# A decoder layer on one core: low halves on GpSimd in pieces of 256 columns, sums over partitions in fp32r

## The chip, the cores and the metric

The kernel runs on one core of a Trainium2 chip. The metric is the device time of one execution in microseconds; for each kernel the median of its runs is taken. The engines are named as in the profile: PE is TensorE, PEld its weight loads, DVE is VectorE, ACT is ScalarE, POOL is GpSimd, SP is SyncE.

## The reference

One layer of a decoder over 512 tokens of width 1024, batch 1, in float32: a gated mixer of NSA sparse attention (8 query heads, 2 key heads) and chunked GLA (4 heads), cross-attention to 256 memory tokens, a gated FFN with a three-tap convolution (width 2816), RMS norms between them and at the end. What the change touches:

```
def rms_norm(x, g):
    y = x * lax.rsqrt(jnp.mean(x * x, axis=-1, keepdims=True) + RMS_EPS)
    return y * g

# GLA: the decay of each key, from a rank-16 product; the norm of each head's output
log_a = jax.nn.log_sigmoid(a_low @ w_alpha2 + b_alpha) / 16.0     # (512,16) @ (16,256)
b = jnp.cumsum(log_a in chunks of 64)
...
o = o * lax.rsqrt(jnp.mean(o * o, axis=-1, keepdims=True) + RMS_EPS) * norm_g
```

## The kernel before

Activations lie transposed: 128 features on the partitions, 512 tokens in the free dimension. A product in float32 accuracy is made of three passes of fp32r matmuls (`mm3`, lines 160 to 162): each operand is split into a high half, its value rounded to fp32r, and a low half, the rest; the passes are high by high, high by low and low by high. A pass of 128 by 512 is one PE instruction.

**Weights.** All weights come as 141 blocks of 128 by 1024 in the order of use. `load_raw` (L126) issues a block's DMA on SP into one of 3 buffers. `convert` makes the two halves: the high half by a copy on ACT (L140), the low half by a subtraction (L141) on the engine that `lo_engine` names at that time. That is DVE at first; DVE and GpSimd in turn from L363 on (projections); DVE again from L452; GpSimd alone from L545 on (NSA and GLA stages with the dense products that fill them); DVE again from L882 (mixer's output and all behind it). Of the 141 blocks GpSimd makes 29. `take` converts two blocks ahead of the one in use.

**Splits of activations** are a copy on ACT (L165) and a subtraction on DVE (L166), by `split`.

**Stages.** First the projections ("proj"), then "nsa": for each of 8 pairs of key head and 128 queries, `nsa_scores` makes scores on PE, the row maxima on DVE, exponentials on ACT and the factors on DVE; `nsa_values` transposes and multiplies. Dense work that depends on none of it is put between them from the list `fillers` (stage name "fill"). The first filler is `gla_r(0)` with `gla_decay`. Then "gla": `gla_qk`, `gla_keys`, `gla_att`, `gla_states`, `gla_out` and `gla_norm` for 4 heads, again with fillers between them (`nsa_part`). Then "mix", "mkv", "wout", "xat", "xo", "up", "down", almost pure dense products.

**Order.** The source gives the semaphores and a priority; the order of the instructions within each engine is made by a list scheduler before the run, which places an instruction when its inputs are ready by its own estimates. Each engine then runs its list in that order. Dependences are kept by region of a tile: a matmul on columns 0 to 127 of a block waits for what wrote these columns.

**Sums over partitions.** A sum over the feature axis is a matmul with a 128 by 128 matrix of ones. `rstd_rows` (L237) does it for the norms ahead of "xat" and "up" (512 columns) and for the last norm (384 columns), `gla_norm` (L833) for each of the 4 GLA heads (512 columns): seven sums, each one fp32 matmul on the fp32 sum of squares. The sum of squares is collected by `add_square`: the square on ACT (L214), the addition on GpSimd (L224). In `gla_out` the square is L828 on ACT.

**The decay gate.** `gla_decay` transposes the 16 low-rank columns (L411), copies them from PSUM on DVE (L413), multiplies them in two fp32 matmuls of 16 by 512 (L418, m = 0 and 1), and goes on with L420 to L431 on ACT and DVE. Other DVE work in the same stretch: L316 and L332 (low halves of queries and keys), L603 (scaled row maxima), L627 (compressed scores times factor), L620 (factors on scores).

Of the kernel before, what the change touches and what calls it, by code (L numbers as in the profile page):

```python
# [9 lines left out]
F32 = mybir.dt.float32  # L10
F32R = mybir.dt.float32r
U32 = mybir.dt.uint32
AF = mybir.ActivationFunctionType
ALU = mybir.AluOpType
AX = mybir.AxisListType

P = 128
T = 512
# [40 lines left out]
def layer_kernel(ctx: ExitStack, tc: tile.TileContext, xT, memT, W, small, const, gfin, out, out_t, order):  # L59
    nc = tc.nc  # L60
# [5 lines left out]
    def sb(shape, dtype, tag, bufs):  # L66
        uid[0] += 1
        return pool.tile(shape, dtype, name=f"{stage[0]}_{tag}_{uid[0]}", tag=tag, bufs=bufs)
# [10 lines left out]
    def s_(dtype=F32):  # L79
        return sb([P, T], dtype, "s", SB)  # L80

    def t_(dtype=F32):
        return sb([P, T], dtype, "t", TB)
# [3 lines left out]
    def bank(tag):  # L87
        uid[0] += 1
        return psum.tile([P, T], F32, name=f"{stage[0]}_ps_{tag}_{uid[0]}", tag=tag, bufs=BANKS[tag])
# [14 lines left out]
    def C(name):  # L104
        a, b = CO[name]
        return cst[:, a:b]

    def S(name):
        a, b = SM[name]
        return sm[:, a:b]  # L110
# [7 lines left out]
    def halves(i):  # L118
        return [slice(0, T), slice(T, 1024)] if i < 4 else [slice(0, 1024)]

    def load_raw(upto):
        while emitted[0] <= min(upto, NBLK - 1):
            i = emitted[0]
            r = sb([P, 1024], F32, "raw", 3)
            for c in halves(i):
                nc.sync.dma_start(r[:, c], W[i][:, c])  # L126
            raws[i] = r
            emitted[0] += 1

    def convert(upto):  # L130
        while emitted[1] <= min(upto, NBLK - 1):
            i = emitted[1]
            load_raw(i + RAW_AHEAD)
            r = raws.pop(i)
            lo = lo_engine[i % len(lo_engine)]
            if i < NBLK - 8:
                wh = sb([P, 1024], F32R, "wh", 3)
                wl = sb([P, 1024], F32R, "wl", 3)
                for c in halves(i):
                    nc.scalar.activation(wh[:, c], r[:, c], AF.Copy)  # L140
                    lo.tensor_tensor(wl[:, c], r[:, c], wh[:, c].bitcast(F32), op=ALU.subtract)  # L141
                convs[i] = (wh, wl)
            else:
                tile_ = s_ if i < NBLK - 5 else g_
                convs[i] = []
                for c in (slice(0, T), slice(T, 1024)):
                    wh, wl = tile_(F32R), tile_(F32R)
                    nc.scalar.activation(wh, r[:, c], AF.Copy)
                    lo.tensor_tensor(wl, r[:, c], wh.bitcast(F32), op=ALU.subtract)
                    convs[i].append((wh, wl))  # L150
            emitted[1] += 1
# [12 lines left out]
    def split(h, l, src):  # L164
        nc.scalar.activation(h, src, AF.Copy)  # L165
        nc.vector.tensor_sub(l, src, h.bitcast(F32))  # L166
# [39 lines left out]
    def gain_split(k, src, gain):  # L206
        h, l = g_(F32R), g_(F32R)
        scaled_split(h, l, src, gain[:, k:k + 1])
        return h, l
# [16 lines left out]
    def rsqrt(dst, src, scale, refine=False):  # L226
        nc.scalar.activation(dst, src, AF.Sqrt, scale=scale, bias=C("eps"))
        nc.vector.reciprocal(dst, dst)
        if refine:
            v = sb([P, 4], F32, "newton", 2)[:, :dst.shape[-1]] if dst.shape[-1] <= 4 else t_()[:, :dst.shape[-1]]  # L230
            nc.vector.scalar_tensor_tensor(v, src, EPS / scale, dst, op0=ALU.add, op1=ALU.mult)
            nc.vector.scalar_tensor_tensor(v, v, -0.5 * scale, dst, op0=ALU.mult, op1=ALU.mult)
            nc.vector.scalar_tensor_tensor(dst, v, 1.5, dst, op0=ALU.add, op1=ALU.mult)

    def rstd_rows(sqacc, n=T, tag="o", refine=False):
        ps = bank(tag)
        nc.tensor.matmul(ps[:, :n], C("ones"), sqacc, start=True, stop=True)  # L237
        r = sb([P, T], F32, "rstd", 2)[:, :n]
        rsqrt(r, ps[:, :n], 1.0 / 1024, refine)
        return r  # L240
# [32 lines left out]
    ps = bank("o")  # L273
# [6 lines left out]
    for k in range(KT):  # L280
        r = s_()
# [3 lines left out]
            load_raw(k // 2)  # L285
    nc.sync.dma_start(cst, const)
    nc.sync.dma_start(sm[:, SM_GAINS:], small[:, SM_GAINS:])
    for k in range(KT):
        xg.append(gain_split(k, xr[k], S("ln_mix")))
        if k % 2 == 0 and k < 6:  # L290
            convert(k // 2)
        if k > 0:
            add_square(sqs, xr[k - 1], eng=nc.vector)
# [75 lines left out]
    for b0, nk in ((0, 3), (3, 3), (6, 2)):  # L369
        w = take(("BB", b0, nk))  # L370
        for j in range(nk):
            k = b0 + j
            c = slice(j * BW, (j + 1) * BW)
# [34 lines left out]
    def gla_decay():  # L408
        alT = bank("pt")
        for t in range(4):  # L410
            nc.tensor.transpose(alT[0:16, t * P:(t + 1) * P], alpha[t], C("ident"))  # L411
        als = t_()
        nc.vector.tensor_copy(als[0:16], alT[0:16])  # L413
        zs = []
        az = sb([P, 2, T], F32, "raw", 3)
        for m in range(2):
            ps = bank("pt")
            nc.tensor.matmul(ps, S("walpha")[0:16, m * P:(m + 1) * P], als[0:16], start=True, stop=True)  # L418
            z = t_()
            nc.scalar.activation(z, ps, AF.Identity, bias=S("b_alpha")[:, m:m + 1])  # L420
            nc.vector.scalar_tensor_tensor(az[:, m], z, -1.0, z, op0=ALU.mult, op1=ALU.max)
            zs.append(z)
        nc.scalar.activation(az, az, AF.Exp, scale=-1.0)
        nc.scalar.activation(az, az, AF.Ln, bias=1.0)
        for m in range(2):
            z = zs[m]
            nc.vector.scalar_tensor_tensor(z, z, 0.0, az[:, m], op0=ALU.min, op1=ALU.subtract)
            cs = g_()
            for c in range(8):
                v = slice(c * 64, c * 64 + 64)  # L430
                nc.vector.tensor_tensor_scan(cs[:, v], C("ones")[:, 0:64], z[:, v], 0.0, op0=ALU.mult, op1=ALU.add)  # L431
            cum[m] = cs
# [35 lines left out]
    for kv in range(2):  # L468
        nc.tensor.matmul(vps[0:31, kv * 64:(kv + 1) * 64], gTs[:, 62 + kv * 31:62 + (kv + 1) * 31], S("w2v"),
                         start=True, stop=True)  # L470
# [220 lines left out]
    for t in range(4):  # L691
        h, l = s_(F32R), s_(F32R)
# [114 lines left out]
    def gla_out(m, a, st, q2, a2):  # L807
        hd = 2 * m + a
        es = slice(hd * P, (hd + 1) * P)
        po = t_()  # L810
        for u in range(2):

            ps = bank(("o", "sc")[u]).rearrange("p (a n) -> p a n", a=2)
            for t in (2 * u, 2 * u + 1):
                ts = slice(t % 2 * P, (t % 2 + 1) * P)
                nc.tensor.matmul(ps[:, :, ts], vb[t][0][:, es], a2[u][:, :, ts], start=True, stop=False)
                nc.tensor.matmul(ps[:, 0, ts], vb[t][1][:, es], a2[u][:, 0, ts], start=False, stop=False)
                for c in (2 * t, 2 * t + 1):
                    if c == 0:
                        continue  # L820
                    cs = slice(c % 4 * 64, (c % 4 + 1) * 64)
                    s = st[(c - 1) // 4][:, (c - 1) % 4 * P:((c - 1) % 4 + 1) * P]
                    nc.tensor.matmul(ps[:, :, cs], s, q2[u][:, :, cs], start=False, stop=c % 2 == 1)
            pu = po[:, u * 256:(u + 1) * 256]
            nc.scalar.activation(pu, ps[:, 1], AF.Copy)
            nc.vector.tensor_add(pu, ps[:, 0], pu)
        sq = t_()
        nc.scalar.activation(sq, po, AF.Square)  # L828
        return hd, po, sq

    def gla_norm(hd, po, sq):
        pn = bank("pt")
        nc.tensor.matmul(pn, C("ones"), sq, start=True, stop=True)  # L833
        rs = t_()
        rsqrt(rs, pn, 1.0 / 128)
        og = t_()
        nc.vector.scalar_tensor_tensor(og, po, S("norm_g"), sr[hd], op0=ALU.mult, op1=ALU.mult)
        nc.vector.scalar_tensor_tensor(og, og, 0.5, rs, op0=ALU.mult, op1=ALU.mult)
        h, l = g_(F32R), g_(F32R)
        split(h, l, og)  # L840
        OG[hd] = (h, l)
# [31 lines left out]
    for k in range(KT):  # L873
        mr = t_()[:, :MEM]
        nc.sync.dma_start(mr, memT[:, k, :])
        hl = sb([P, 2, MEM], F32R, "s", SB)
# [9 lines left out]
    for n in range(0, 8, 2):  # L886
        th = [merge(C_MG, n, t_), merge(C_MG, n + 1, t_)]
        for j in range(2):
            ps = branch("w_branch_gla", OG, n + j)
            nc.vector.scalar_tensor_tensor(th[j], th[j], 1.0, ps, op0=ALU.add, op1=ALU.mult)  # L890
            nc.gpsimd.tensor_tensor(th[j], pm[n + j], th[j], op=ALU.add)
            if n < 4:
                x = pair()
                h, l = x[:, 0], x[:, 1]
            else:
                h, l = g_(F32R), g_(F32R)
# [9 lines left out]
    for hd in range(4):  # L906
        ps = pk[hd] if hd < 2 else dense8(("A", "w_xkv", hd * P), memg, MEM)
        kf = t_()[:, :MEM]
        nc.vector.tensor_mul(kf, ps[:, :MEM], rm)
        hl = sb([P, 2, MEM], F32R, "g", GB)  # L910
# [6 lines left out]
    for n in range(8):  # L917
        xr = t_()
        nc.sync.dma_start(xr, xT[:, n, :])
        ps = dense8(("A", "w_out", n * P), mix)  # L920
        r = g_()
# [9 lines left out]
    for t in range(2):  # L931
        h, l = g_(F32R), g_(F32R)
# [147 lines left out]
    for n in range(8):  # L1080
        ps = acc()
        for k in range(HF):
# [3 lines left out]
            c = slice(j % 8 * P, (j % 8 + 1) * P)  # L1086
# [42 lines left out]
    for n in range(4, 8):  # L1129
        ps = bank(("sc", "pt", "acc", "pt")[n - 4])[:, head]  # L1130
# [24 lines left out]
    for i, (h, c) in enumerate(((0, slice(0, T)), (1, slice(0, 256)), (1, slice(256, T)))):  # L1155
        ps = bank(("pt", "o", "sc")[i])[:, c]
# [141 lines left out]
```

## Time and profile before

| | us |
|---|---|
| runs shown | 873.52, 875.91, 876.02 |
| median | 875.91 |
| the profiled execution | 875.57 |
| its span on the core | 873.5 |
| PE busy | 853.2 |
| DVE busy | 557.7 |
| ACT busy | 419.1 |
| POOL busy | 214.2 |

The span runs from the first to the last instruction on the core; the execution's own time is 2.1 us longer. Busy time of PE counts each matmul to its modelled end, so neighbours overlap. A row of the timeline has the start, the duration (of several merged instructions from the first start to the last end), the engine, line, operation, tile written and tiles read, the shape and the count; in brackets stands idle time just ahead, with what ended it. An fp32 matmul shows as two entries. A DVE duration includes the time in which the instruction had been issued and could not yet start.

### The profile page before, as it was taken

What the parts mean: (1) busy time and instruction counts of PE and PEld (TensorE: products, weight loads), DVE (VectorE), ACT (ScalarE), POOL (GpSimd) and SP (SyncE); (2) the same over time, 40 slices, a digit from 0 to 9 for tenths busy, and PEclk for the clock granted to TensorE, in tenths of its full rate; (3) what the DMA queues carried; (4) which work ended last, traced back from release to release, by engine and by line L of the source; (5) the groups of instructions that cost most, each with busy time, mean ns of one, the idle gap of its engine ahead of it and who ended that gap; (6) DMA issues with size and microseconds to landing.
All of it is one profiled execution on the core that took longest, in us unless ns stands there. A gap on an engine that the chain in (4) does not pass through costs nothing.

```text
span 873.5 us, 11086 instructions
## 1 busy us (share of the span) xinstructions
PE 853.2 (98%) x4174; PEld 708.0 (81%) x4174; DVE 557.7 (64%) x908; ACT 419.1 (48%) x731; POOL 214.2 (25%) x160
## 2 busy tenths in 40 slices
PE   9999989999998999999999999999999999999996
PEld 6987777777786878898888788888888888888996
DVE  7576977998858378454487669665533465565324
ACT  7466767798445455344446535433311233334311
POOL 1373444344333314112300222111100111112121
PEclk9999999999999999999999999999999999999999
DMA  8333221002221232244341132322222223222302
GB/s 293 116 123 97 73 73 49 25 2 73 67 78 49 96 116 103 96 169 146 123 143 49 48 121 74 120 96 97 97 97 96 97 86 108 90 97 102 121 25 97
DMA packets 26406, 83.58 MB, mean 96 GB/s; under 512 B 3056, under 2 KB 5104, under 8 KB 26352
## 3 DMA queue, kind: packets, MB, share of 16 engines
q1 hardware_dynamic: 26064, 82.58, 27.2%
q8 instruction: 33, 0.54, 0.3%
q10 hardware_dynamic: 288, 0.28, 0.1%
q14 instruction: 21, 0.17, 0.1%
HBM read 80.76 MB, written 2.10 MB: 95 GB/s over the span
## 4 chain that ended last, share of the span: by engine, by line
PE 88%; DVE 7%; ACT 3%; issue 1%; POOL 1%; ACTq 0%; POOLq 0%
PE up_ps_sc L161 4%; PE up_ps_sc L160 4%; PE up_ps_sc L162 4%; PE fill_ps_acc L160 3%; PE fill_ps_acc L161 3%; PE fill_ps_acc L162 3%; PE up_ps_pt L160 3%; PE up_ps_pt L161 3%; PE up_ps_pt L162 3%; PE up_ps_acc L161 2%; PE up_ps_acc L160 2%; PE up_ps_acc L162 2%; PE nsa_ps_o L644 2%; PE down_ps_sc L162 2%; PE nsa_ps_pt L650 2%; PE down_ps_sc L161 2%
## 5 line engine op out<-in xcount | busy, mean ns | idle before, releaser
L1068 POOL TENSOR_TENSOR up_s<-up_s,up_s 128x512 f32<-128x512 f32 x22 | 35.8, 1630 | 259.6 <-ACT up_wh L140 207.7
L140 ACT ACTIVATE up_wh<-up_raw 128x1024 fp32r<-128x1024 f32 x40 | 42.5, 1062 | 64.9 <-PE up_ps_sc L161 33.0
L141 DVE TENSOR_TENSOR up_wl<-up_raw,up_wh 128x1024 fp32r<-128x1024 f32 x40 | 62.8, 1569 | 16.0 <-ACT up_wh L140 15.9
L141 POOL TENSOR_TENSOR fill_wl<-fill_raw,fill_wh 128x1024 fp32r<-128x1024 f32 x16 | 38.5, 2407 | 48.7 <-ACT fill_wh L140 46.7
L160 PE MATMUL up_ps_sc<-xo_g,up_wh 128*128 128x512 f32 x124 | 48.7, 393 | 0.0
L162 PE MATMUL up_ps_sc<-xo_g,up_wl 128*128 128x512 f32 x124 | 48.3, 389 | 0.0
L161 PE MATMUL up_ps_sc<-xo_g,up_wh 128*128 128x512 f32 x124 | 48.3, 389 | 0.0
L160 PE MATMUL up_ps_pt<-xo_g,up_wh 128*128 128x512 f32 x104 | 40.6, 390 | 0.0
L162 PE MATMUL up_ps_pt<-xo_g,up_wl 128*128 128x512 f32 x104 | 40.5, 389 | 0.0
L161 PE MATMUL up_ps_pt<-xo_g,up_wh 128*128 128x512 f32 x104 | 40.5, 389 | 0.0
L612 ACT ACTIVATE nsa_s<-nsa_s,nsa_nm 128x128 f32<-128x128 f32 (+3 forms) x64 | 34.2, 536 | 11.7 <-DVE nsa_nm L603 11.7
L160 PE MATMUL fill_ps_acc<-in_g,fill_wh 128*128 128x512 f32 x96 | 38.3, 399 | 0.2 <-DVE fill_t L529 0.2
L161 PE MATMUL fill_ps_acc<-in_g,fill_wh 128*128 128x512 f32 x96 | 38.3, 399 | 0.0
L162 PE MATMUL fill_ps_acc<-in_g,fill_wl 128*128 128x512 f32 x96 | 38.1, 396 | 0.0
L162 PE MATMUL up_ps_acc<-xo_g,up_wl 128*128 128x512 f32 x88 | 34.2, 389 | 0.0
L161 PE MATMUL up_ps_acc<-xo_g,up_wh 128*128 128x512 f32 x88 | 34.2, 389 | 0.0
L160 PE MATMUL up_ps_acc<-xo_g,up_wh 128*128 128x512 f32 x88 | 34.2, 389 | 0.0
L1064 ACT ACTIVATE up_s<-up_s 128x512 f32<-128x512 f32 x22 | 13.8, 632 | 40.2 <-DVE up_s L1062 40.2
L140 ACT ACTIVATE down_wh<-down_raw 128x1024 fp32r<-128x1024 f32 x9 | 9.5, 1061 | 39.4 <-PE down_ps_sc L161 17.5
L224 POOL TENSOR_TENSOR xo_g<-xo_g,xo_t 128x512 f32<-128x512 f32 x7 | 12.3, 1756 | 63.8 <-ACT xo_g L214 61.3
L140 ACT ACTIVATE fill_wh<-fill_raw 128x1024 fp32r<-128x1024 f32 x16 | 16.9, 1057 | 21.9 <-PE fill_ps_acc L161 14.9
L160 PEld LDWEIGHTS up_ps_sc<-xo_g,up_wh 128*128 128x128 f32 x124 | 23.3, 188 | 5.1 <-issue 0.2
(943 smaller groups left out, 2716.0 us busy)
## 6 DMA issues: line engine op xcount, KB each, us to landing
up_raw<-in_w SPq DMA_DIRECT2D x44, 512.0 KB, 3.2
fill_raw<-in_w SPq DMA_DIRECT2D x20, 512.0 KB, 3.2
down_raw<-in_w SPq DMA_DIRECT2D x18, 512.0 KB, 3.2
proj_raw<-in_w SPq DMA_DIRECT2D x14, 512.0 KB, 3.3
mix_raw<-in_w SPq DMA_DIRECT2D x12, 512.0 KB, 3.3
mkv_raw<-in_w SPq DMA_DIRECT2D x8, 512.0 KB, 3.2
wout_raw<-in_w SPq DMA_DIRECT2D x8, 512.0 KB, 3.4
in_s<-in_xT SPq DMA_DIRECT2D x8, 256.0 KB, 5.4
```

The lines of the kernel that those rows point to most:

```text
L140: nc.scalar.activation(wh[:, c], r[:, c], AF.Copy)
L141: lo.tensor_tensor(wl[:, c], r[:, c], wh[:, c].bitcast(F32), op=ALU.subtract)
L160: nc.tensor.matmul(ps, w[0], x[0], start=first, stop=False)
L161: nc.tensor.matmul(ps, w[0], x[1], start=False, stop=False)
L162: nc.tensor.matmul(ps, w[1], x[0], start=False, stop=last)
L224: eng.tensor_tensor(state[0], state[0], q, op=ALU.add)
L612: nc.scalar.activation(s[:, :w], s[:, :w], AF.Exp, scale=sl, bias=nm[:, c:c + 1], accum_out=sums[:, c:c + 1])
L644: nc.tensor.matmul(po, v, x, start=j == 0 and x is parts[0], stop=j == last and x is parts[-1])
L650: nc.tensor.transpose(pt[:, g * P:(g + 1) * P], srcs[g], C("ident"))
L1064: nc.scalar.activation(cv, cv, AF.Gelu_apprx_tanh)
L1068: nc.gpsimd.tensor_tensor(gm, gm, cv, op=ALU.mult)
```

## The change

- `convert` makes a low half on GpSimd in four subtractions of 256 columns each in place of one of 1024. On DVE it stays one.
- Each of the seven sums is done in two fp32r passes: the sum of squares is split by `split` (ACT copy, DVE subtraction) into two new buffers, one of each kind for all seven, and each half is multiplied by a copy of the ones in fp32r, made once on GpSimd.
- `gla_decay` packs three row groups into the 128 rows of a single fp32r product: the high half, the low half and the high half again of the low-rank columns against the high, the high and the low half of the weights. The rest of the rows is cleared by two fills on GpSimd. Two fp32r matmuls of 128 by 512 take the place of the two fp32 matmuls of 16 by 512; two more ACT copies and one DVE subtraction prepare the weights, and ACT copy, DVE subtraction and a second ACT copy stand where the one DVE copy L413 was.

```diff
+    def pieces(c, eng):
+        n = 256 if eng is nc.gpsimd else c.stop - c.start
+        return [slice(a, a + n) for a in range(c.start, c.stop, n)]
...
                     nc.scalar.activation(wh[:, c], r[:, c], AF.Copy)
-                    lo.tensor_tensor(wl[:, c], r[:, c], wh[:, c].bitcast(F32), op=ALU.subtract)
+                    for d in pieces(c, lo):
+                        lo.tensor_tensor(wl[:, d], r[:, d], wh[:, d].bitcast(F32), op=ALU.subtract)
...
+    ones = sb([P, P], F32R, "ones", 1)
+
+    def sum_split(sq, n=T):
+        h, l = sb([P, T], F32R, "sqh", 1)[:, :n], sb([P, T], F32R, "sql", 1)[:, :n]
+        split(h, l, sq)
+        return h, l
+
+    def sum_rows(ps, h, l):
+        nc.tensor.matmul(ps, ones, h, start=True, stop=False)
+        nc.tensor.matmul(ps, ones, l, start=False, stop=True)
+
     def rstd_rows(sqacc, n=T, tag="o", refine=False):
+        hl = sum_split(sqacc, n)
         ps = bank(tag)
-        nc.tensor.matmul(ps[:, :n], C("ones"), sqacc, start=True, stop=True)
+        sum_rows(ps[:, :n], *hl)
...
+    nc.gpsimd.tensor_copy(ones, C("ones"))
...
-        als = t_()
-        nc.vector.tensor_copy(als[0:16], alT[0:16])
+        als, wa = t_(F32R), sb([P, 256], F32R, "walpha", 1)
+        nc.gpsimd.memset(als.bitcast(F32), 0.0)
+        nc.gpsimd.memset(wa.bitcast(F32), 0.0)
+        nc.scalar.activation(wa[0:16], S("walpha")[0:16], AF.Copy)
+        nc.scalar.activation(wa[32:48], S("walpha")[0:16], AF.Copy)
+        nc.vector.tensor_sub(wa[64:80], S("walpha")[0:16], wa[0:16].bitcast(F32))
+        split(als[0:16], als[32:48], alT[0:16])
+        nc.scalar.activation(als[64:80], alT[0:16], AF.Copy)
...
-            nc.tensor.matmul(ps, S("walpha")[0:16, m * P:(m + 1) * P], als[0:16], start=True, stop=True)
+            nc.tensor.matmul(ps, wa[:, m * P:(m + 1) * P], als, start=True, stop=True)
...
         nc.scalar.activation(sq, po, AF.Square)
-        return hd, po, sq
-
-    def gla_norm(hd, po, sq):
+        return hd, po, sum_split(sq)
+
+    def gla_norm(hd, po, hl):
         pn = bank("pt")
-        nc.tensor.matmul(pn, C("ones"), sq, start=True, stop=True)
+        sum_rows(pn, *hl)
```

## Rows read from the trace of the kernel before

**Rows 1.** The page: span, then busy us, share and instructions of two engines

```profile
span 873.5 us, 11086 instructions
...
PE 853.2 (98%) x4174; PEld 708.0 (81%) x4174; DVE 557.7 (64%) x908; ACT 419.1 (48%) x731; POOL 214.2 (25%) x160
```

**Rows 2.** Waits of PE: who waited for whom, us in total, times, longest

```profile
PE nsa_ps_o L644 <- DVE nsa_t L669: 3.2, 4, 1.9
...
PE nsa_ps_sc L562 <- DVE nsa_mx L596: 1.1, 1, 1.1
...
PE gla_ps_sc L746 <- DVE gla_t L166: 1.0, 1, 1.0
...
PE proj_ps_acc L162 <- POOL proj_wl L141: 0.5, 1, 0.5
```

**Rows 3.** Timeline of POOL and DVE, 73 to 77 us

```profile
73.35 2.38 POOL L141 TENSOR_TENSOR fill_wl<-proj_raw,fill_wh 128x1024 fp32r<-128x1024 f32 x1 [3.36 <-ACT fill_wh L140]
...
73.89 2.40 DVE L316 TENSOR_TENSOR proj_g<-proj_t,proj_g 64x512 fp32r<-64x512 f32 x1
```

**Rows 4.** Timeline, 105 to 110 us

```profile
106.63 2.43 POOL L141 TENSOR_TENSOR fill_wl<-fill_raw,fill_wh 128x1024 fp32r<-128x1024 f32 x1
106.72 2.48 DVE L627 TENSOR_TENSOR proj_cm<-proj_cm,nsa_cf 128x124 f32<-128x124 f32 x1
```

**Rows 5.** Stretches: us; PE, PEld, DVE, ACT, POOL busy; PEclk; DMA; GB/s

```profile
109.20:111.00 1.80, 0.00 (x0) 0.00 (x0) 1.75 (x7) 0.05 (x1) 0.00 (x0) 1.00 0.50 141
112.50:115.80 3.30, 3.30 (x11) 2.64 (x10) 2.08 (x6) 2.64 (x10) 0.39 (x1) 0.50 0.02 5
```

**Rows 6.** Timeline of POOL, DVE and PE: two further places, 147 and 263 us

```profile
147.94 2.38 POOL L141 TENSOR_TENSOR fill_wl<-fill_raw,fill_wh 128x1024 fp32r<-128x1024 f32 x1 [1.97 <-ACT proj_pc L165]
...
149.11 1.24 DVE L603 TENSOR_TENSOR nsa_nm<-nsa_mx,in_cst 128x12 f32<-128x12 f32 x1
...
151.25 0.47 PE L644 MATMUL nsa_ps_o<-nsa_pth,proj_g 128*128 128x512 f32 x1 [0.84 <-DVE nsa_t L669]
...
263.38 2.43 DVE L166 TENSOR_TENSOR gla_g<-gla_t,gla_g 128x512 fp32r<-128x512 f32 x1 [0.41 <-ACT gla_g L165]
```

**Rows 7.** Groups of POOL by shape: count, busy us, mean ns, idle before

```profile
L141 POOL TENSOR_TENSOR fill_wl<-fill_raw,fill_wh 128x1024 fp32r<-128x1024 f32 x16 | 38.5, 2407 | 48.7 <-ACT fill_wh L140 46.7 <-ACT proj_pc L165 2.0
...
L505 POOL TENSOR_TENSOR fill_g<-fill_g,fill_t 128x512 f32<-128x512 f32 x2 | 2.6, 1312 | 2.3 <-DVE fill_g L504 2.3
```

**Rows 8.** Timeline of POOL and DVE in the mix stage, 341 to 346 us

```profile
341.83 1.30 POOL L891 TENSOR_TENSOR mix_t<-fill_g,mix_t 128x512 f32<-128x512 f32 x1 [2.07 <-DVE mix_t L890]
...
342.53 1.68 DVE L141 TENSOR_TENSOR mix_wl<-mix_raw,mix_wh 128x1024 fp32r<-128x1024 f32 x1
...
343.08 2.28 POOL L891 TENSOR_TENSOR mix_t<-fill_g,mix_t 128x512 f32<-128x512 f32 x1
```

**Rows 9.** Timeline of PE at the sum ahead of "xat" and at L418

```profile
441.21 1.02 PE L237 MATMUL xat_ps_o<-wout_g,in_cst 128*128 128x512 f32 x2
...
442.29 0.39 PE L161 MATMUL xat_ps_acc<-wout_g,mkv_wh 128*128 128x512 f32 x1
442.52 0.40 PE L162 MATMUL xat_ps_acc<-wout_g,mkv_wl 128*128 128x512 f32 x1
...
86.10 1.98 PE L418 MATMUL fill_ps_pt<-fill_t,in_sm 16*128 16x512 f32 x4
```

**Rows 10.** Line L828: ns min, median, max of its four instructions

```profile
L828 ACT ACTIVATE gla_t<-gla_t x4: 612/624/633, 246.2 to 309.2; 128x512 f32<-128x512 f32 x4
```

**Rows 11.** Groups of DVE, 60 to 312 us, by shape: two-input subtraction

```profile
L166 DVE TENSOR_TENSOR gla_s<-gla_s,gla_s 64x512 fp32r<-64x512 f32 x4 | 2.7, 687 | 0.1
```

**Rows 12.** Timeline of PE and POOL where sums stand: second GLA head, "xat"

```profile
261.75 1.00 PE L791 MATMUL gla_ps_sc<-gla_g,gla_g 128*128 128x128 f32 x8
...
263.93 1.12 PE L833 MATMUL gla_ps_pt<-gla_t,in_cst 128*128 128x512 f32 x2 [0.88 <-ACT gla_t L828]
...
432.47 1.80 POOL L224 TENSOR_TENSOR wout_g<-wout_g,wout_t 128x512 f32<-128x512 f32 x1 [3.65 <-ACT wout_t L214]
```

## Prediction

> **What bounds the kernel now.** I read the page first. PE is busy for 853.2 of 873.5 us and no other engine is near [rows 1]; so work taken off PE counts in full where PE does not wait, and anything else counts only where PE stands still. Next the waits of PE, to see where that is. They are short and few, and nearly all lie between 40 and 310 us, in the projections, NSA and GLA, where low halves are made on GpSimd: four waits for L669 (3.2 us in total, the longest 1.9), one for L596 (1.1), one for a low half on DVE (1.0), one for a low half on GpSimd (0.5) [rows 2]. Then the timeline just ahead of each of these waits, DVE beside POOL. The reader is to see one pattern. L316 was issued at 73.89, while GpSimd's block ran from 73.35 to 75.73, and it ended at 76.29: 0.56 us of work behind 1.8 us of standing [rows 3]. L627, 124 columns, took 2.48 us beside the block of 106.63 to 109.06 [rows 4]; L603, 12 columns, 1.24 us beside that of 147.94 [rows 6]; the L166 at 263.38, 2.43 us [rows 6] where the like take 0.69 [rows 11]. All four read two operands from SBUF. They stand until GpSimd's instruction ends, whatever their own size. [...]
>
> **Pieces of 256 columns.** A block of 1024 takes 2.41 us on GpSimd and an instruction of 512 columns 1.31 [rows 7]. The line through both has 2.14 ns a column and 0.22 us of fixed cost; 256 columns then take 0.76 us, four 3.05. Bounds for a piece: 0.60, a quarter of the block, if nothing is fixed, and 1.31 if it is no shorter than 512 columns; I take 0.76, since both rows lie on the same kind of instruction. The 29 blocks then cost GpSimd 29 x 0.64 = 19 us more, on an engine that is busy for a quarter of the span [rows 1]; it costs PE nothing unless L604, L606 or L626, which queue behind the blocks on GpSimd, become the last to arrive.
>
> What the pieces give depends on DVE getting in between two of them. In the mix stage two GpSimd instructions follow each other without a gap, from 341.83 to 343.13 and from 343.08; the DVE subtraction issued at 342.53 ended at 344.21, well ahead of the second one's end at 345.36, and the second took 2.28 us against 1.30 for the first [rows 8]. DVE got in, and GpSimd stood. So a standing DVE instruction waits for the rest of one piece: L316, issued 0.54 into its block, for 0.2 us in place of 1.8; L627, issued 0.09 into it, for 0.7 in place of 2.3; L603, issued 1.17 into it, for 0.35 in place of 1.2; the L166 at 263.38 for under 0.76 in place of about 1.7. PE's waits behind these four are 1.1 [rows 2], 1.9 [rows 2, 5], 0.84 [rows 6] and 1.0 [rows 2]; bounded by the smaller of the wait and what is saved ahead of it, they give 1.1 + 1.6 + 0.84 + 1.0 = 4.5 us. The wait for the low half itself goes too, since the first two slices of 128 columns need the first piece alone: 0.5 [rows 2]. Sum 5.0 us. What is late next: the DVE instructions behind the freed one meet the next piece in turn, up to 0.7 us each, and GpSimd's own block is stretched by each that gets in. So I take two thirds, 3.4 us, between 0 and 5.0.
>
> [...]
>
> **The clock.** At half clock, 3.3 us hold 1.65 us of work [rows 5], so the fall cost at least 1.6 us. The other waits of [rows 2], 1.1 us and less, are followed by no such stretch. With the wait at 109 us down to 0.3, I take the whole 1.6 as given back; bounds 0 and 1.6.
>
> **fp32r passes.** From the start of the fp32 sum at 441.21 to the second fp32r pass behind it at 442.29 are 1.08 us, and fp32r passes follow each other by 0.23 [rows 9]; so the fp32 sum holds PE for 0.85 us, two fp32r passes for 0.46. Six sums of 512 columns give 6 x 0.39 = 2.3 us, the one of 384 columns three quarters of 0.39, 0.3. The gate's two matmuls are the same two entries each (four in 1.98 us [rows 9]): 1.70 against 2 x 0.23 = 0.46, that is 1.2. Together 3.9 us off PE; bounds 3.5 (where a weight load shows) and 4.2 (with the whole 1.98 counted).
>
> **Splitting the sums.** Each split adds a copy on ACT, 0.62 us like the square in front of it [rows 10], and a two-input subtraction on DVE, 0.69 [rows 11]: 1.3 us between the sum of squares and its matmul, seven times. Where it is hidden: ahead of "xat" the last addition of squares ended at 434.27 [rows 12] and the sum stood on PE at 441.21 [rows 9], 7 us later, with dense products between; "up" has a like distance; the first and third GLA head have fillers of 24 matmuls and more in between. The second and fourth head have not: there PE already waited 0.88 us at 263.93 for the square [rows 12], and 1.3 us is added in front. PE's order is set by estimated readiness, not by the source: L791 of the next head, written behind the sum, ran at 261.75 ahead of it [rows 12]; so a later sum lets other matmuls pass. For each of the two heads between 0 and 1.3; I take half, 1.3 for both, and 0.3 for the last norm, whose square sum arrives late too: 1.6 us, between 0 and 2.9. The two buffers have one copy each, but the sums are many us apart.
>
> **The decay gate's preparation.** One DVE copy becomes ACT copy, DVE subtraction, and a second ACT copy beside it: some 0.6 us more on the way to L418. The weights' part and the two fills need nothing of that chain and go at zero under GpSimd's and ACT's idle time; if they came late, the whole chain up to L431 would, by up to their 1.3 us (two such copies). Against it, the chain is shorter by the 1.2 us of L418. I take zero.
>
> **Sum.** -3.4 - 1.6 - 3.9 + 1.6 = -7.3 us. The profiled execution took 875.57, so 868.3 us; its neighbours at 875.91 and 876.02 and the one at 873.52 show that the base is within 0.4 of the median. The bounds of the terms taken together (the waits given back at a third to all) give 865 to 872.6 for this case.
>
> **The rivals.**
>
> First, waits pass on: NSA is so tightly coupled that a DVE instruction freed here meets a piece there, or GpSimd's longer blocks make L604, L606 or L626 late. Then only the passes and the splits count: 875.57 - 3.9 + 1.6 = 873.3. For it: the alternation in [rows 8], which slowed GpSimd's second instruction by 1.0 us. Against: each of the four stalls ends right ahead of PE's wait.
>
> Second, and on the other side: the splits stand too late in the queues of ACT and DVE. If at "xat" and "up" the split stood in source order, behind the work of the product ahead of it (one conversion and one subtraction of 1024 columns and a few more), PE would stand for about 2.5 us at each, and a standstill of 1.9 us was enough for the clock's fall of 1.6 [rows 5]: 8.2 us; with the full 1.3 at the five others, 6.5. Then 875.57 - 8.9 + 14.7 = 881.4. It decides against the change once the seven sums stand for more than 8.9 + 2.6 = 11.5 us, 1.6 us each. Against it: L791 [rows 12], an order by readiness.
>
> Third, DVE does not get in between pieces of one block. The four stalls would then last for 3.05 in place of 2.41, 0.64 x 4 = 2.6 us longer: 873.3 + 2.6 = 875.9, no change.
>
> **How the numbers follow.** Within 0.3% (2.6 us) this kernel's runs tell nothing apart. My forecast has 0.66, of which 0.02 is within 0.3%. The first rival has 0.16 (0.07 faster, 0.09 the same, since 873.3 lies beside the border), the second 0.11 (0.09 slower, 0.02 the same), the third 0.07 (0.05 the same, 0.02 slower). Faster 0.71, the same 0.18, slower 0.11. The range runs from 863.5, where the other short waits of NSA go as well, to 875.5; outside it lie the second rival, half of the third and a small rest below, 0.19.
>
> **What would show it.** Right: pieces of about 0.76 us, DVE's L316, L627 and L603 under 1.0, no stretch at clock 0.50 near 112 us, and PE's waits between 40 and 310 us down by half; sums as pairs 0.23 apart; PE's busy time down by about 4 us. Wrong: pieces near 1.3 us; DVE still standing through a block; waits of a microsecond and more on a sum's low half in "gla", "xat" or "up"; ACT or DVE waiting for L604, L606 or L626; a new standstill of 2 us and a new stretch at half clock.

## The result, and the profile after

Slower: 879.63 us, median of ten executions (876.18 to 883.53), beside 873.93 for the kernel before on the same chip; ratio 1.0057, 95% interval 1.004 to 1.0075. By the ratio that is 5.0 us lost (5.7 between the medians) where 7.3 were forecast to be won, and the time lies above the range. The profiled execution took 880.23, its span is 878.4; by span the loss is 4.9 us. The profiled executions of two experiments below (sums alone, and before in the changed kernel's order) took 3002 and 1063 us, for a reason that no run shows; no times are read from their traces, and all comparisons leave them out.

In the lines below L147 is L141 of before, L171 and L172 are L165 and L166, L631 and L632 are L606 and L607, L637 is L612, L652 is L627, L669 is L644, L694 is L669 and L443 is L418.

First the page of the changed kernel, its span and its first line of busy time:

```profile
span 878.4 us, 11188 instructions
PE 856.5 (98%) x4172; PEld 710.9 (81%) x4172; DVE 551.6 (63%) x916; ACT 425.9 (48%) x742; POOL 238.8 (27%) x250
```

PE is busier than before [rows 1], though work was taken off it. The work did go. Here are two timeline rows of a GLA head's sum, the two passes of which start 0.22 apart, and the row of the gate's two products, 0.62 in place of 1.98 [rows 9]:

```profile
262.18 0.39 PE L249 MATMUL gla_ps_pt<-gla_sqh,in_ones 128*128 128x512 f32 x1
262.40 0.39 PE L250 MATMUL gla_ps_pt<-gla_sql,in_ones 128*128 128x512 f32 x1
...
89.77 0.62 PE L443 MATMUL fill_ps_pt<-fill_t,fill_walpha 128*128 128x512 f32 x2
```

The pieces do what they were to do. The first row is the page's group of most of them (busy, mean ns of one); then comes the timeline of GpSimd's block at 105 and of DVE's product of the compressed scores (124 columns) beside it:

```profile
L147 POOL TENSOR_TENSOR fill_wl<-fill_raw,fill_wh 128x256 fp32r<-128x256 f32 x64 | 49.2, 798 | 45.7 <-ACT fill_wh L145 45.7
```

```profile
105.14 2.88 POOL L147 TENSOR_TENSOR fill_wl<-fill_raw,fill_wh 128x256 fp32r<-128x256 f32 x4
...
105.24 0.81 DVE L652 TENSOR_TENSOR proj_cm<-proj_cm,nsa_cf 128x124 f32<-128x124 f32 x1
```

A piece takes 0.80 us. DVE's L652, issued 0.10 into the block, ended at 106.05, while the block ran to 108.02; the same instruction stood for 2.48 in before [rows 4]. The wait of PE behind it is gone.

Then the waits of PE (total, times, longest), those of [rows 2] with their successors:

```profile
PE nsa_ps_o L669 <- DVE nsa_ptl L172: 3.5, 4, 1.3
PE nsa_ps_o L669 <- ACT nsa_pth L171: 3.3, 3, 1.9
...
PE nsa_ps_sc L606 <- DVE nsa_cf L641: 0.9, 1, 0.9
PE gla_ps_sc L771 <- ACT gla_t L171: 0.9, 1, 0.9
...
PE nsa_ps_o L669 <- DVE nsa_t L694: 0.4, 1, 0.4
```

The largest wait of before, on L694's like, is down from 3.2 to 0.4; others have come, most of them at L669 for the halves of a transposed tile. Last, the granted clock in four stretches (PEclk), the first of them PE's longest standstill:

```profile
119.50:121.35 1.85, 0.00 (x1) 0.01 (x1) 0.43 (x3) 1.85 (x8) 0.00 (x0) 1.00 0.00 0
122.40:129.10 6.70, 5.81 (x21) 4.32 (x19) 5.27 (x14) 3.02 (x5) 5.00 (x7) 0.50 0.14 39
207.70:211.00 3.30, 3.30 (x13) 2.71 (x11) 1.10 (x2) 2.19 (x4) 3.30 (x6) 0.50 0.00 0
272.60:279.30 6.70, 6.70 (x22) 4.93 (x19) 6.61 (x9) 1.81 (x4) 0.75 (x2) 0.50 0.23 81
```

PE ran 16.7 us at a granted clock of 0.50, in before 3.3 [rows 5]. That makes up, as an estimate, the balance of the two profiled executions: the passes -3.9; PE's idle gaps of 0.05 us and more, added up over each trace, 13.7 for 11.9, so +1.8; half of 13.4 more us at half clock, +6.7 (in the last of these stretches two fill passes started 0.43 us apart, at 274.44 and 274.87; at clock 1.00 two started 0.23 apart, at 117.03 and 117.26); together +4.6 beside 4.9 by span. What the balance does not say is why PE stands still in other places than before.

### The profile page after: what moved, and what is told of

Its sections match the earlier page's. It is cut to its first block, busy times and chain, and to the rows that moved or that the text cites. A ratio compares the mean times of both kernels' runs of the same rounds, so it can differ in the third digit from the quotient of the medians.

```text
span 878.4 us, 11188 instructions
## 1 busy us (share of the span) xinstructions
PE 856.5 (98%) x4172; PEld 710.9 (81%) x4172; DVE 551.6 (63%) x916; ACT 425.9 (48%) x742; POOL 238.8 (27%) x250
## 4 chain that ended last, share of the span: by engine, by line
PE 84%; ACT 6%; DVE 5%; POOL 2%; issue 1%; DMA 1%; ACTq 0%; DVEq 0%; POOLq 0%
PE up_ps_sc L166 4%; PE up_ps_sc L167 4%; PE up_ps_sc L168 4%; PE fill_ps_acc L167 3%; PE fill_ps_acc L166 3%; PE fill_ps_acc L168 3%; PE up_ps_pt L166 3%; PE up_ps_pt L167 3%; PE up_ps_pt L168 3%; PE up_ps_acc L166 2%; PE up_ps_acc L167 2%; PE up_ps_acc L168 2%; PE nsa_ps_o L669 2%; PE down_ps_sc L168 2%; ACT nsa_s L637 2%; PE down_ps_sc L167 2%
## 5 line engine op out<-in xcount | busy, mean ns | idle before, releaser
L1093 POOL TENSOR_TENSOR up_s<-up_s,up_s 128x512 f32<-128x512 f32 x22 | 38.8, 1766 | 256.1 <-ACT up_wh L145 204.2
L147 DVE TENSOR_TENSOR up_wl<-up_raw,up_wh 128x1024 fp32r<-128x1024 f32 x40 | 59.4, 1484 | 15.5 <-ACT up_wh L145 15.5
L147 POOL TENSOR_TENSOR fill_wl<-fill_raw,fill_wh 128x256 fp32r<-128x256 f32 x64 | 49.2, 798 | 45.7 <-ACT fill_wh L145 45.7
L166 PE MATMUL up_ps_sc<-xo_g,up_wh 128*128 128x512 f32 x124 | 48.3, 389 | 0.0
L166 PE MATMUL up_ps_pt<-xo_g,up_wh 128*128 128x512 f32 x104 | 40.5, 389 | 0.0
L166 PE MATMUL fill_ps_acc<-in_g,fill_wh 128*128 128x512 f32 x96 | 38.9, 405 | 0.2 <-DVE fill_t L554 0.2
L637 ACT ACTIVATE nsa_s<-nsa_s,nsa_nm 128x128 f32<-128x128 f32 (+3 forms) x64 | 34.1, 535 | 7.4 <-DVE nsa_nm L628 7.4
L166 PE MATMUL up_ps_acc<-xo_g,up_wh 128*128 128x512 f32 x88 | 34.2, 389 | 0.0
L651 POOL TENSOR_SCALAR nsa_s<-nsa_s,nsa_cf 128x384 f32<-128x384 f32 (+2 forms) x16 | 18.6, 1174 | 35.8 <-ACT nsa_pth L171 17.0
```

Of the source, the lines that this page charges most:

```text
L147: lo.tensor_tensor(wl[:, d], r[:, d], wh[:, d].bitcast(F32), op=ALU.subtract)
L166: nc.tensor.matmul(ps, w[0], x[0], start=first, stop=False)
L637: nc.scalar.activation(s[:, :w], s[:, :w], AF.Exp, scale=sl, bias=nm[:, c:c + 1], accum_out=sums[:, c:c + 1])
L651: nc.gpsimd.tensor_scalar(b, b, cf[:, 2, g:g + 1], None, op0=ALU.mult)
L1093: nc.gpsimd.tensor_tensor(gm, gm, cv, op=ALU.mult)
```

## The experiments

Each ran beside the kernel before on the same chip; kernels of different rows of the table are compared by their ratios. "Row" in the text is a place in the list of PE's instructions, of 4075 in before.

| run | what | median us | ratio to before, 95% |
|---|---|---|---|
| e1 | pieces alone | 871.29 | 0.9967 (0.9954 to 0.998) |
| e2 | sums alone | 873.01 | 0.9981 (0.9969 to 0.9992) |
| e3 | gate alone | 884.5 | 1.012 (1.0104 to 1.0136) |
| e4 | sums and gate | 885.34 | 1.012 (1.0096 to 1.0143) |
| e5 | one copy on ACT | 883.13 | 1.0097 (1.0084 to 1.011) |
| e6 | gate prepared apart | 879.2 | 1.0052 (1.0039 to 1.0064) |
| e7 | pieces and sums | 869.51 | 0.9945 (0.9933 to 0.9957) |
| e8 | all, gate prepared apart | 874.32 | 1.0002 (0.9988 to 1.0016) |
| e9 | before, in after's order | 886.89 | 1.0147 (1.0129 to 1.0166) |
| e10 | gate alone, in before's order | 876.47 | 1.0022 (1.0011 to 1.0032) |
| e11 | all, in e7's order | 872.5 | 0.9982 (0.9973 to 0.9991) |
| e12 | e8, in e7's order | 870.45 | 0.9952 (0.9937 to 0.9967) |
| e13 | all, one swap in GpSimd's list | 873.35 | 0.9989 (0.9978 to 1.0001) |
| e14 | all, ACT's lists changed | 888.65 | 1.0156 (1.0141 to 1.0171) |

### The parts (e1 to e4)

Each is before with some hunks of the change's diff and no others: e1 `pieces`, e2 `sum_split` and `sum_rows`, e3 the hunk of `gla_decay`, e4 the last two together.

```diff
 e1 -                    lo.tensor_tensor(wl[:, c], r[:, c], wh[:, c].bitcast(F32), op=ALU.subtract)
    +                    for d in pieces(c, lo):
    +                        lo.tensor_tensor(wl[:, d], r[:, d], wh[:, d].bitcast(F32), op=ALU.subtract)
 e3 -        nc.vector.tensor_copy(als[0:16], alT[0:16])
    +        split(als[0:16], als[32:48], alT[0:16])
    +        nc.scalar.activation(als[64:80], alT[0:16], AF.Copy)
```

> The kernel before with the pieces of 256 columns alone; the order of PE, ACT and DVE is then that of before, instruction by instruction. Theory of the order (the loss comes from the list that the new sums and the gate give NSA): 4 to 6 us faster than before, L627 and L603 under 1.0 us, no stretch at clock 0.50 near 112 us. Theory of the pieces (they hold up L604 and L606 on GpSimd and by them the exponentials): 4 to 6 us slower, with new waits of PE in NSA. Theory of the passes (less fp32 work lets the clock fall): as the theory of the order.

> The seven sums alone in two fp32r passes, blocks whole, the gate as before. Theory of the order: 1.5 to 2.7 us faster (2.6 of passes, less some waits in GLA), NSA as before with its fall of the clock at 112 us. Theory of the pieces: the same. Theory of the passes: slower by 1 to 3 us, with a stretch at clock 0.50 in GLA, near 270 us, where the fp32 sum of the second head stood.

> The decay gate alone as one packed fp32r product, blocks whole, sums as before. Theory of the order: 3 to 7 us slower although PE has 1.3 us less to do, with new waits of PE of a microsecond and more in NSA and more time at clock 0.50. Theory of the pieces and theory of the passes: 0 to 1.5 us faster.

> The sums and the gate, blocks whole: the changed kernel without its pieces; PE's order is that of the changed kernel but for a few instructions. Theory of the order: 3 to 10 us slower than before, as slow as the changed kernel (5.7) or slower, since the pieces were the part that helped. Theory of the pieces: 2 to 4 us faster than before. Theory of the passes: 2 to 6 us slower.

The loss is the gate's: alone it costs 10.5 us, though its product holds PE for 1.4 less. Pieces and sums gain. The theory of the order has the sides right, but not all sizes: e1 gained 2.9 where 4 to 6 were expected, e3 lost 10.5 where 3 to 7 were, and e4 10.5 where 3 to 10 were. Pieces bring more beside the gate: on top of e4 they make 5.5 us (0.0063 of ratio). The lists of instructions fit this. Pieces alone leave those of PE, ACT and DVE as they are; the sums change PE's list first at row 1249, behind NSA; the gate changes it from row 466, its own product, on to row 1107, through all of NSA into GLA.

### What in the gate (e5, e6), and the change without it (e7, e8)

e5 is before with one instruction on another engine. e6 is the gate edit with its operand prepared apart; e8 the whole change with that (there the cleared buffer is the one of the sums' high half, which the sums use only after NSA).

```diff
 e5 -        nc.vector.tensor_copy(als[0:16], alT[0:16])
    +        nc.scalar.activation(als[0:16], alT[0:16], AF.Copy)
 e6 +    ALS = sb([P, T], F32R, "als", 1)                 # with the first loads
    +    nc.gpsimd.memset(ALS.bitcast(F32), 0.0)
    ...
    +        nc.vector.tensor_copy(als[0:16], alT[0:16])
    +        nc.vector.tensor_sub(als[32:48], alT[0:16], als[0:16].bitcast(F32))
    +        nc.gpsimd.tensor_copy(als[64:80], als[0:16].bitcast(F32))
```

> Edit: the kernel before, with one instruction on another engine: the copy of the 16 low-rank rows from PSUM (L413) on ACT in place of DVE; the gate's fp32 products stay. In PE's list the gate's product moves from row 466 to row 472 (with the whole gate edit: row 480). Theory of the queue: in before this copy ran on DVE at 82.70, straight behind the transposes; on ACT it stands behind the exponentials that run to 83.8 (with the gate alone its split ran there only at 85.31). The product is late by part of what the gate edit makes it late, so part of that loss: 875 to 884, centre 878, slower than before's 874.1. Theory of the fp32r product itself (the 128-row form, the fills, the weights' halves cost the time): none of them is here, so 874.1 within 0.3%. Theory of the re-made order as such (before's order is a lucky one, and any other is worse): 878 to 886, as with the gate alone.

> Edit: the kernel before with the gate's fp32r product, prepared in another way: its packed operand has a buffer of its own that GpSimd clears at the start, DVE makes the high and the low half straight from PSUM, GpSimd the second high half from SBUF, and GpSimd makes the weights' halves; ACT has no part in it. In PE's list the product stands at row 458 (before 466, gate edit as changed 480). Theory of the queue: the product is no longer late, and two passes of 0.23 stand in place of 0.85 each; 874.1 - 1.2 = 872.9, between 869 and 874.5. Theory of the fp32r product itself: as with the gate alone, 884. Theory of the re-made order as such (the list differs from before's in almost as many places as with the gate alone): 878 to 886.

> Edit: the change without its gate edit: pieces of 256 columns and the seven sums in fp32r, the gate's product in fp32 as before. If the parts add up, 874.1 - 2.8 (pieces alone) - 1.0 (sums alone) = 870.3, between 868.5 and 872. If the pieces save more beside another order, as they seem to do beside the gate edit (5.7 us there), 867 to 869. Theory that sums and pieces hinder each other: 873 or more.

> Edit: the whole change, with the gate prepared as in the run before the last one (own cleared buffer, halves on DVE and GpSimd, ACT without a part). Theory of the queue: the sum of the parts, 874.1 - 2.8 - 1.0 - 1.2 = 869.1, between 866 and 872, and some 10 us under the changed kernel's 879.6. Theory of the fp32r product itself or of the re-made order: 876 or more.

One copy on ACT, with all of the old work, costs 8.5 us. In its timeline, ACT's last exponential of this stage, then the copy, then PE's fp32 product:

```profile
83.32 0.39 ACT L612 ACTIVATE nsa_s<-nsa_s,nsa_nm 128x128 f32<-128x128 f32 x1
...
85.25 0.57 ACT L413 ACTIVATE fill_t<-fill_ps_pt 16x512 f32<-16x512 f32 x1
...
87.28 1.98 PE L418 MATMUL fill_ps_pt<-fill_t,in_sm 16*128 16x512 f32 x4
```

The product started 1.2 us later than in before [rows 9], and 8.5 us were lost. The fp32r product is not in this run, so the loss does not need it; and 1.2 us of lateness by itself is far from 8.5. e6 speaks against lateness as the whole cause too: its product ran at 84.18, ahead of before's 86.10 [rows 9], and it still lost 4.5 us. The theory of the queue missed e6 by 5.7 us and e8 by some 5. Its list too is another one, and PE stands still in a new place, 2.12 us ahead of 100.09:

```profile
84.18 0.70 PE L426 MATMUL fill_ps_pt<-in_als,fill_walpha 128*128 128x512 f32 x2
...
100.09 0.63 PE L652 MATMUL nsa_ps_o<-nsa_ptl,proj_g 128*128 128x512 f32 x1 [2.12 <-DVE nsa_ptl L166]
```

e7, the change without its gate edit, has the lowest ratio of all: 4.8 us under before, near the sum of its two parts (2.9 and 1.7).

### Work and order taken apart (e9 to e12)

Here each engine's list is pinned by edges between neighbours, which order the issue and wait for nothing; so the same work can run in another kernel's order.

```diff
     with tile.TileContext(nc) as tc:
         layer_kernel(tc, *args, order)
+        pin(nc, tc)
...
+    for names in ...:                                    # one list for PE, ACT, DVE and POOL each
+        chain = [traced[f"I-{n}"] for n in names if f"I-{n}" in traced]
+        for a, b in zip(chain, chain[1:]):
+            tc.add_manual_dep(b, a.name, mybir.DependencyInfo(mybir.DependencyClass.NoSync, ...), reason="order")
```

> Edit: none of the change; the kernel before, instruction for instruction (blocks of 1024, fp32 sums, fp32 gate product), but every engine's list put in the order of the changed kernel, by edges that order the issue and wait for nothing. Theory of the order (the loss lies in the lists, not in the work): the time of sums with gate (885.3, nearly this order with whole blocks) plus the 3.9 of the fp32 passes that are back: 885 to 891. Theory that the new instructions themselves cost the time: none is here, so 874.1 within 0.3%.

> Edit: the gate edit alone, as in the change (its split on ACT and DVE, its fills on GpSimd; alone it took 884.5), but all instructions that the kernel before has too stand in before's order on every engine; only the gate's own new ones are placed freely, its product at row 481 of PE's list as with the gate alone. Theory of the order: 874.1 - 1.2 = 872.9, between 871.5 and 876. Theory of lateness (the product that comes 2.5 us later by ACT's split holds up what follows, whatever the order): 877 to 885, as before by up to all of the 10.5.

> Edit: the changed kernel, instruction for instruction, with every engine's list in the order of pieces with sums and the gate as before (869.5); only the gate's own new instructions are placed freely, its product at row 481. Theory of the order: 869.5 - 1.2 = 868.3, between 867 and 871, some 11 under the changed kernel in its own order (879.6), and near the 868.3 forecast. Theory of lateness: 873 to 880.

> Edit: as the run before, but with the gate's operand in a buffer cleared at the start and its halves made on DVE and GpSimd, so that its product stands at row 458 of PE's list and ACT has no part in it. Theory of the order: 868.3, between 866.5 and 870, the same as the run before. Theory of lateness: faster than the run before by 4 us and more.

e9 shows what order alone can cost: with none of the change's instructions and only its order, before takes 12.8 us more by the ratio (its executions: 886.0, 886.9 and 888.7). That order includes the late place of the gate's product; e10 and e11 keep that place late and put only the rest back. e10 then costs 1.9 us where the same edit in its own order (e3) cost 10.5. And e11, with all of the change's instructions in e7's order, is 6.6 us under the changed kernel (0.9982 beside 1.0057). The rest of the gate's price is its lateness: e11 stays 3.2 us above e7 (0.9982 beside 0.9945) and so falls between its two forecasts (up to 871, from 873 on), and e10 stays 1.9 above before where 1.2 below was expected. In e11's timeline, PE's two standstills and DVE's wait ahead of them:

```profile
90.34 0.91 PE L675 MATMUL nsa_ps_pt<-in_cst,nsa_s 128*128 128x128 f32 x5 [0.55 <-ACT fill_t L445]
93.09 0.47 PE L603 MATMUL nsa_ps_sc<-in_pair,proj_g 128*128 128x512 f32 x1 [1.85 <-DVE proj_cm L590]
...
90.31 1.30 DVE L446 SCALAR_TENSOR_TENSOR fill_raw<-fill_t 128x512 f32<-128x512 f32 x2 [2.52 <-ACT fill_t L445]
```

DVE stands for 2.52 us at L446, which takes the gate's product, and the score work queued behind it (L590) lets PE stand for 1.85. With the gate prepared apart, in the same order (e12), the first standstill is gone, the second is down to 0.37 (ahead of 90.83), and 2.6 us are won by the ratios; but e12 is no faster than e7. The gate edit gains nothing that can be measured even so. In its own order the same kernel (e8) loses 4.4 us of that again.

### Which place in the order (e13, e14)

In the trace of the changed kernel, the timeline ahead of PE's longest standstill, by engine: GpSimd, DVE, ACT, PE:

```profile
113.10 2.83 POOL L147 TENSOR_TENSOR fill_wl<-fill_raw,fill_wh 128x256 fp32r<-128x256 f32 x4 [4.72 <-ACT fill_wh L145]
115.89 0.39 POOL L631 TENSOR_TENSOR proj_cm<-proj_cm,nsa_nm 128x124 f32<-128x124 f32 x1
...
113.08 0.16 DVE L628 TENSOR_TENSOR nsa_nm<-nsa_mx,in_cst 128x12 f32<-128x12 f32 x1
...
116.31 0.31 ACT L632 ACTIVATE proj_cm<-proj_cm 128x124 f32<-128x124 f32 x1 [2.33 <-POOL proj_cm L631]
...
120.13 0.60 ACT L637 ACTIVATE nsa_s<-nsa_s,nsa_nm 128x384 f32<-128x384 f32 x1
120.72 1.05 ACT L171 ACTIVATE nsa_pth<-nsa_ps_pt 128x512 fp32r<-128x512 f32 x2
...
121.35 0.50 PE L669 MATMUL nsa_ps_o<-nsa_pth,proj_g 128*128 128x512 f32 x1 [1.86 <-ACT nsa_pth L171]
```

L631 had its input from L628 at 113.24, but a block of four pieces stood ahead of it in GpSimd's list. ACT waited 2.33 us for it at L632, with seven exponentials queued behind that had all they needed, and behind them the copy that PE waited for. None of the seven passed L632: they ran from 116.53 on, one behind the other. The place comes with the gate edit, not with the pieces: in e4, with whole blocks, the block ran at 115.76 for 2.40, L631's like at 118.12, and ACT had waited 1.91.

It is not what every re-made order loses by. e5 lost 8.5 us with this place in good order; its GpSimd rows there, and then PE's two longest standstills, further on:

```profile
114.46 0.40 POOL L606 TENSOR_TENSOR proj_cm<-proj_cm,nsa_nm 128x124 f32<-128x124 f32 x1 [3.76 <-DVE nsa_nm L603]
114.81 2.40 POOL L141 TENSOR_TENSOR fill_wl<-fill_raw,fill_wh 128x1024 fp32r<-128x1024 f32 x1
...
156.10 0.50 PE L644 MATMUL nsa_ps_o<-nsa_pth,proj_g 128*128 128x512 f32 x1 [1.43 <-ACT nsa_pth L165]
...
228.78 0.58 PE L746 MATMUL gla_ps_sc<-gla_s,gla_t 64*128 64x256 f32 x1 [1.69 <-DVE gla_t L795]
```

What makes these two late was not tested.

e13 moves L631 ahead of this one block, in GpSimd's list, and pins the rest as it was. e14 moves L632 behind the eight exponentials in ACT's list, in all eight stages.

```diff
 e13, GpSimd's list, third score stage
+  TENSOR_TENSOR proj_cm<-proj_cm,nsa_nm     (L631)
   TENSOR_TENSOR fill_wl<-fill_raw,fill_wh   (L147, four pieces)
-  TENSOR_TENSOR proj_cm<-proj_cm,nsa_nm     (L631)
```

> Edit: the changed kernel in its own order on every engine, but for one place in GpSimd's list: in the third score stage of NSA the last scaling of the compressed scores (L631) stands ahead of the four pieces of the block that it followed. Theory of this place: ACT's exponentials start 2.3 us earlier, PE's standstill of 1.86 at 119.5 and the next of 0.89 go at least by half (1.4 to 2.7), and the stretch of 6.8 us at half clock behind them goes (3.4): 879.6 less 4.8 to 6.1, so 873.5 to 875. Theory that the loss is spread over the whole order, or that the wait only passes on to the next stage: 878 to 880.

> Edit: the changed kernel in its own order on every engine, but for ACT's list: in each of the eight score stages the exponential of the compressed scores (L632), which waits for GpSimd, stands behind the eight other exponentials (L637) in place of among or ahead of them. Theory that ACT's wait for GpSimd holds the exponentials: as with the one swap, 4.8 to 6.1 less, and up to 2 more from the other stages: 871.5 to 875. Theory that the loss is spread, or lies in the queues of DVE and PE: 878 and more; a loss beyond 880 if DVE's sum over the late exponential (L633) now holds the factors.

The one swap gives 5.9 us (0.9989 beside 1.0057), as much as the theory of this place had it. GpSimd, ACT and PE at the place, and then the granted clock from 100 to 300 us, all of e13:

```profile
113.28 0.39 POOL L631 TENSOR_TENSOR proj_cm<-proj_cm,nsa_nm 128x124 f32<-128x124 f32 x1 [5.02 <-DVE nsa_nm L628]
113.63 2.83 POOL L147 TENSOR_TENSOR fill_wl<-fill_raw,fill_wh 128x256 fp32r<-128x256 f32 x4
...
113.79 0.29 ACT L632 ACTIVATE proj_cm<-proj_cm 128x124 f32<-128x124 f32 x1
...
118.18 1.06 ACT L171 ACTIVATE nsa_pth<-nsa_ps_pt 128x512 fp32r<-128x512 f32 x2
...
121.37 0.50 PE L669 MATMUL nsa_ps_o<-nsa_ptl,proj_g 128*128 128x512 f32 x1 [0.74 <-DVE nsa_ptl L172]
```

```profile
100.00:200.00 100.00, 93.94 (x477) 73.44 (x476) 81.26 (x250) 76.17 (x202) 43.66 (x55) 1.00 0.11 36
200.00:300.00 100.00, 95.51 (x492) 77.12 (x491) 72.02 (x121) 53.80 (x91) 47.57 (x62) 1.00 0.22 74
```

The swap let L632 run 2.5 us earlier; the standstill of 1.86 is gone, and in the profiled execution half clock as well: at 1.00 over each hundred there is no room for even 3 us of it (they would make 0.98), where the changed kernel had 16.7. That is more than the theory of this place says: only the first of the three stretches lay behind it. Since PE's list is the same in both runs, one instruction's start can be set beside the other's. DVE's L628, ahead of the swap, ran at 113.08 and at 112.98 in e13, so up to there the pinning alone cost nothing. PE's L669 of 207.07 ran at 202.34, 4.7 us earlier: that was won at the place. The L771 of 270.16 ran at 264.32, 5.8 earlier, and the span is 7.2 shorter (871.2): the last 2.5 us come behind 207 and 270, where the changed kernel fell to half clock and e13 did not (last section). e14 went the other way, by 8.7 us: its waits of PE and of DVE show why.

```profile
PE nsa_ps_sc L606 <- DVE nsa_mx L609: 4.6, 1, 4.6
PE nsa_ps_o L669 <- DVE proj_pc L172: 3.1, 1, 3.1
...
DVE nsa_sums L633 <- ACT proj_cm L632: 25.7, 8, 5.2
```

DVE's sum over L632's result (L633) kept its place in DVE's list, ahead of row maxima and low halves; there DVE now stood for 25.7 us. The loss by L633 was the case that the expectation gave last. So the wait for GpSimd cost time where it came ahead of ready work (5.9 us, e13); putting L632 behind that work, with DVE's list still keyed to its old place, cost more (8.7, e14).

## Why the prediction was wrong

**Pieces: right, also in size.** Piece and block took 0.80 and 2.83 us (forecast 0.76 and 3.05); pieces alone gave 2.9 us by e1's ratio (forecast 3.4, bounds 0 to 5.0). The third rival falls with the 0.81 of L652: it ended at 106.05, when the first piece of its block had run (from 105.14; the four took 0.73 to 0.77 each) and the block had 2 us to go.

**The clock: wrong as a term, and with it the base.** The forecast starts from the profiled execution, 875.57 us at a mean granted clock of 0.996, and that one has the fall at 112 us. The 17 executions of before beside e5 stand in two groups: eight of 873.7 to 874.0 at 0.997 and 0.998, nine of 874.9 to 876.7 at 0.995 and 0.996. Means of 0.997 and 0.998 leave room, as an estimate over a span of 872 us, for 5.2 and 3.5 us at half clock, and 3.3 of them stand at the end of the profiled execution, where PE has nothing to do (the first row):

```profile
870.20:873.50 3.30, 0.00 (x0) 0.00 (x0) 0.00 (x0) 0.00 (x0) 0.00 (x0) 0.50 0.38 145
...
68.50:71.70 3.20, 2.96 (x8) 1.82 (x6) 2.22 (x3) 3.12 (x5) 1.28 (x2) 0.50 0.70 259
```

So the first group most likely had no fall at 112 us to give back; no trace of one of them shows it. The base was 1.6 us above the median of ten (873.93), about what the term was to win. In e1 the stretch at 112 us was gone, but 3.2 us at half clock stood from 68.5 on (the second row), where the profiled before had none; and e1 was profiled in its slowest execution (873.14 at 0.996; the other four took 870.96 to 871.46 at 0.998). A fall can't be booked to one wait as if it could not turn up elsewhere; the price of 1.6 for one fall was also small beside the 6.7 that the new ones cost.

**Passes and splits: right.** Sums alone were to give -2.6 + 1.6 = -1.0; e2's median is 1.1 under before, by its ratio 1.7. No wait of a microsecond stands at a sum, in "gla", "xat" or "up" (the longest at any of the seven is 0.5): the second rival had the right side and the wrong mechanism, and that its 881.4 lies near the measured time is luck.

**The decay gate's preparation: the step that failed.** "I take zero" rested on two things. One is that the copies run when their inputs are ready. ACT's list put them behind its exponentials; in the trace of the changed kernel:

```profile
84.54 0.39 ACT L637 ACTIVATE nsa_s<-nsa_s,nsa_nm 128x128 f32<-128x128 f32 x1
...
86.48 0.57 ACT L171 ACTIVATE fill_t<-fill_ps_pt 16x512 fp32r<-16x512 f32 x1
86.95 1.04 ACT L145 ACTIVATE fill_wh<-proj_raw 128x1024 fp32r<-128x1024 f32 x1
88.02 0.59 ACT L438 ACTIVATE fill_t<-fill_ps_pt 16x512 fp32r<-16x512 f32 x1
```

Its product followed at 89.77, 3.7 us after before's, though its transposes stood only 1.0 later (82.7 beside 81.7). In a good order the gate edit's net price is 3.2 us (e11 against e7). The other, unsaid, is that the lists around the gate stay as they were. The prediction states that the order is made from estimated readiness, and uses that for one sum only. The re-made lists of NSA cost 6.6 us (after against e11), and taking one block from ahead of one L631 gives back 5.9 (e13), two thirds of it at that place by the traces. The prediction had named that condition ("unless L604, L606 or L626 ... become the last to arrive") and the sign of it ("ACT or DVE waiting for L604, L606 or L626"). Its first rival put it down to longer blocks and priced it at no more than the waits that the pieces were to give back (873.3 in all); it came by the order, with whole blocks too (e4), and cost more.

The terms as measured, by differences of ratios, each good to some 2 us: pieces and sums -4.8, the gate in a good order +3.2, the re-made order +6.6, together +5.0.

What stays open: e9's 12.8 us are more than the 6.6 that the order costs the changed kernel. That pieces soften a bad order would fit e4 and after (10.5 against 5.0), and two standstills of PE in e4, with the same ones in the changed kernel behind them, speak for it:

```profile
161.67 0.50 PE L663 MATMUL nsa_ps_o<-nsa_pth,proj_g 128*128 128x512 f32 x1 [1.44 <-ACT nsa_pth L165]
236.33 0.38 PE L765 MATMUL gla_ps_sc<-gla_s,gla_t 64*128 64x256 f32 x1 [1.69 <-DVE gla_t L814]
...
158.57 0.50 PE L669 MATMUL nsa_ps_o<-nsa_pth,proj_g 128*128 128x512 f32 x1 [0.94 <-ACT nsa_pth L171]
230.35 0.38 PE L771 MATMUL gla_ps_sc<-gla_s,gla_t 64*128 64x256 f32 x1 [0.60 <-DVE gla_t L820]
```

No run puts before with pieces into the changed kernel's order, which would test it.

## What to carry to other kernels

Where a list scheduler makes the order, an edit of one small instruction in a tightly coupled stage is an edit of the whole stage: compare the lists of before and after, engine by engine, before pricing the edit, and look for a long instruction that has come to stand ahead of one on the critical chain. Time the parts of a change alone, since the one worth 1.2 us on paper can eat what the others bring. To tell the price of the work from that of its order, pin one kernel's order on the other's work; two places swapped in one list were worth 5.9 us here.

## What the runs showed of the hardware

The same standstill of PE was followed by a fall of the clock in one run and not in another. In the changed kernel PE stood 1.34 us ahead of 207.07 and 0.89 ahead of 270.16, and a clock of 0.50 followed at 207.7 and 272.6; in e13 the same two waits stand ahead of 202.34 and 264.32, 1.34 and 0.89 us long, and the clock stayed at 1.00:

```profile
202.34 0.50 PE L669 MATMUL nsa_ps_o<-nsa_ptl,proj_g 128*128 128x512 f32 x1 [1.34 <-DVE nsa_ptl L172]
...
264.32 0.51 PE L771 MATMUL gla_ps_sc<-gla_s,gla_t 64*128 64x256 f32 x4 [0.89 <-ACT gla_t L171]
```

The executions of the changed kernel also differ among themselves with the clock: 876.2 us at a mean granted clock of 0.995, 883.5 at 0.984. What decides between the two, no run here shows.
